# Samples' features finished block by block at the end of two SwiGLU down phases, and where their norms' products stand

## The chip, the cores and the metric

The kernel runs on one core of a Trainium2 chip. The core has TensorE (PE; PEld is its weight load), VectorE (DVE), ScalarE (ACT), GpSimd (POOL) and SyncE (SP, which only issues transfers), each with its own in-order instruction queue, and 16 DMA engines that all queues share. The metric is the device time of one execution in microseconds; the time before is the median of three runs.

## The reference

One decoder layer over 1024 prompt tokens and 8 samples of 4 tokens, in fp32. Three sublayers, each with a norm that is scaled and shifted per sequence, and a gated residual; then a final norm:

```python
h = _modulate(_rms(x, p["ffn1_norm"]), sh1, sc1)
x = x + 0.5 * g1[:, None, :] * _swiglu(h, p["ffn1_w_gate"], p["ffn1_w_up"], p["ffn1_w_down"])
h = _modulate(_rms(x, p["mix_norm"]), sh2, sc2)
m, new = _mixer(h, conv[l], hst[l], shift[l], wkv[l], p)
x = x + g2[:, None, :] * m
h = _modulate(_rms(x, p["ffn2_norm"]), sh3, sc3)
x = x + 0.5 * g3[:, None, :] * _swiglu(h, p["ffn2_w_gate"], p["ffn2_w_up"], p["ffn2_w_down"])
...
y = _rms(x, final_norm)
```

`_swiglu(h, wg, wu, wd)` is `(silu(h @ wg) * (h @ wu)) @ wd`; the model has 1024 features and 2816 hidden ones. `_rms` divides each token by the root of the mean of its squared features and multiplies by a vector. The gates g1, g2, g3 are one vector for the prompt and one for each of the eight samples. `_mixer` is a parallel pair of recurrences (RG-LRU and RWKV-7) between two projections, w_in and w_out.

## The kernel before

**Tiling.** x lies in the core's memory as features by tokens: 8 blocks of 128 features, and 1056 columns, of which the last 32 are the samples' tokens. In the phases spoken of here the columns are taken in three pieces, piece 0 and 1 of 384 columns and piece 2 of 288, that is 256 prompt columns and the 32 of the samples. Every product is fp32 made of three products of split operands (lines 61 to 63 in `mm3`): a value is split by ACT into a rounded high part (line 46) and by DVE into the rest (line 47).

**Order.** The program is written in Python and a planner puts each engine's instructions in order, by its own estimates of time and by priority, which is the written order unless a `high_priority` says otherwise. Inside `in_order(engine)` the engine keeps the written order. So PE's order in the last group of a down phase is as written, while DVE, ACT and POOL are planned. In most of the mixer PE is planned too.

**A down phase (`down`, line 475).** The hidden features come in groups of two or three blocks of 128 from DRAM. For each group, piece and block `ob` of output features, PE makes nine products (six in small groups) into one PSUM tile, `pd`. Then `acc_x` (lines 460 to 466) adds it to x on DVE: line 463 for the prompt columns, with the prompt's gate. The samples' 32 columns are only summed up in `sacc`, without a gate (line 466), since each sample has its own gate. In the last group the pieces go 0, 1, 2, and when all blocks of piece 2 are done, `add_samples` multiplies all of `sacc` (8 x 32 columns) by the gates (line 472) and adds it to x (line 473).

**The norm behind it (`rstd_steps`, line 166)** is a generator in three steps, so that its few products on PE can be put between those of the next piece. Step one: ACT squares each feature block (lines 173 and 176), and an adder engine (POOL in ffn1; in ffn2 POOL for pieces 0 and 1, DVE for piece 2) sums the blocks into `acc` (line 177; the profile names it nacc). For piece 2 this takes the 256 prompt columns, and the samples' columns come separately: one square over 8 x 32 columns (line 180) and one reduction on DVE (line 181). Step two: eight narrow products sum over features (line 185, `nps`), then a root on ACT (line 187) and a reciprocal on DVE (line 188). Step three: eight products spread the result over 128 rows (line 192, `npb`), copied to memory by ACT (line 194, `nrs`).

`done(ci)` runs step one as soon as a piece's blocks are written; the next two steps are taken while the next piece's blocks are written, behind the block numbers in `marks`. The line

```python
if pend and ob in marks[i - 1]:
    next(pend, None)
```

stands in the loop over blocks. The default `marks=((1, 3), (2, 4))` holds in ffn1's phase. The call of ffn2's phase gives its own, `((2, 4), (5, 7))`. Steps two and three for piece 2 of ffn1 are taken in the mixer's first projection, behind its second and third product group (`pj`).

**What follows.** In ffn1, step three is followed by the mixer's norm: DVE scales (line 436, `nt`), ACT adds the shift and rounds (line 443), DVE takes the rest (line 444); the samples' columns go through lines 455 to 457. Beside these, the projection's weights arrive by DMA through one buffer (`wr`) and are split. x is also stored to DRAM from POOL's queue (line 1316, `dx_move`). In ffn2 the final norm follows: `final` (line 1675) scales piece 0 on DVE (line 1694), piece 1 on POOL (ACT multiplies by the norm's vector, line 1685, and POOL by `nrs`, line 1692), and piece 2 on both, five blocks on DVE and three on POOL. After every second block an output DMA is issued, from SP and ACT in turn (line 1696). `add_samples` is also called at the end of the mixer's output projection (`w_out_end`).

Of the kernel before, what the change touches and what calls it, by code (L numbers as in the profile page):

```python
# [8 lines left out]
F32 = mybir.dt.float32  # L9
F32R = mybir.dt.float32r  # L10
AF = mybir.ActivationFunctionType
ALU = mybir.AluOpType
PSUM = bass.MemoryType.PSUM

D, NP, NB, TS = 1024, 1024, 8, 4
T = NP + NB * TS
KD = D // 128
# [4 lines left out]
PL = NP - 768  # L22
# [16 lines left out]
def trunk(tc, a):  # L39
    nc = tc.nc  # L40
# [93 lines left out]
    x = None  # L134
# [31 lines left out]
    def rstd_steps(ci, ps_, sp, adder=nc.vector):  # L166
        c, n = PIECES[ci]
        b = n // 4
        np_ = n if ci != 2 else PL
        acc = sp.tile([128, n], F32, tag="acc", name="nacc")  # L170
        for k in range(KD):
            if k == 0:
                nc.scalar.activation(acc[:, 0:np_], x[:, 0, c:c + np_], AF.Square)
            else:
                sq = sp.tile([128, n], F32, tag="sq", name="nsq")
                nc.scalar.activation(sq[:, 0:np_], x[:, k, c:c + np_], AF.Square)
                adder.tensor_tensor(acc[:, 0:np_], acc[:, 0:np_], sq[:, 0:np_], op=ALU.add)
        if ci == 2:
            sq = sp.tile([128, n], F32, tag="sq", name="nsqs")[:, 0:256].rearrange("p (k t) -> p k t", k=KD)
            nc.scalar.activation(sq, x[:, :, NP:T], AF.Square)  # L180
            nc.vector.tensor_reduce(acc[:, PL:n].unsqueeze(2), sq.rearrange("p k t -> p t k"), axis=mybir.AxisListType.X, op=ALU.add)
        yield
        ps = ps_([b, 4], "nps")
        for s in range(4):
            nc.tensor.matmul(ps[:, s:s + 1], acc[:, b * s:b * s + b], ones, start=(s == 0), stop=(s == 3))
        rn = sp.tile([128, 4], F32, tag="rn", name="rn")
        nc.scalar.activation(rn[0:b], ps, AF.Sqrt, bias=eps[0:b])
        nc.vector.reciprocal(rn[0:b], rn[0:b])
        yield
        pb = ps_([128, n], "npb")  # L190
        for s in range(4):
            nc.tensor.matmul(pb[:, b * s:b * s + b], rn[0:b, s:s + 1].to_broadcast([b, 128]), ident[0:b, 0:b], start=True, stop=True)
        rs = sp.tile([128, n], F32, tag="rs", name="nrs")
        nc.scalar.activation(rs, pb, AF.Copy)
        yield rs
# [264 lines left out]
    def acc_x(ps, ci, ob, g, gs):  # L460
        c, n = PIECES[ci]
        np_ = n if ci != 2 else PL
        nc.vector.scalar_tensor_tensor(x[:, ob, c:c + np_], ps[:, 0:np_], g[:, ob, 0:1], x[:, ob, c:c + np_],  # L463
                                       op0=ALU.mult, op1=ALU.add)
        if np_ < n:
            nc.vector.tensor_tensor(sacc[:, ob, :], ps[:, np_:n], sacc[:, ob, :], op=ALU.add)

    sacc = const.tile([128, KD, 32], F32, name="sacc")

    def add_samples(g):  # L470
        sv = sacc.rearrange("p k (b s) -> p k b s", b=NB)
        nc.vector.tensor_tensor(sv, sv, g[:, :, 1:9].unsqueeze(3).to_broadcast([128, KD, NB, TS]), op=ALU.mult)
        nc.vector.tensor_tensor(x[:, :, NP:T], x[:, :, NP:T], sacc, op=ALU.add)

    def down(pre, gc, dH, hid, more, done, hot=False, main_done=None, pieces=(0, 1, 2), marks=((1, 3), (2, 4))):
        nc.vector.memset(sacc, 0.0)
        started = ExitStack()
        started.enter_context(in_order(nc.sync))
        for gi, (g0, g1) in enumerate(GROUPS):
            if gi == 2:  # L480
                started.close()
            last = g1 == NH
            if last and main_done:
                main_done()
            from_ = (more, more) if gi % 2 == 0 else (hid, PL_["w"])
            hid_t, wd = [], []
            for m in range(g0, g1):
                r = PL_["wr"].tile([128, T], F32, "wr", "wr")
                nc.sync.dma_start(r, dH[m])
                hid_t.append([from_[0].tile([128, T], F32R, t, t) for t in ("fh", "fl")])  # L490
                split(r, *hid_t[-1])
                wd.append(weight(a[pre + "_w_down"][m], from_[1]))
            pend = None
            with in_order(nc.tensor) if last else ExitStack():
                for i, ci in enumerate(pieces if last else (2, 1, 0)):
                    c, n = PIECES[ci]
                    with tc.high_priority(3000) if last and hot and i > 0 else ExitStack():
                        for ob in range(KD):
                            ps = F([128, n], "pd")
                            mm3(ps, [(wd[j][0][:, 128 * ob:128 * ob + 128], wd[j][1][:, 128 * ob:128 * ob + 128],  # L500
                                      hid_t[j][0][:, c:c + n], hid_t[j][1][:, c:c + n]) for j in range(g1 - g0)])
                            acc_x(ps, ci, ob, gc, None)
                            if pend and ob in marks[i - 1]:
                                next(pend, None)
                    if last:
                        for _ in pend or ():
                            pass
                        with tc.high_priority(3000) if ci == 2 else ExitStack():
                            if ci == 2:
                                add_samples(gc)  # L510
                            pend = done(ci)
                            next(pend)
        return pend
# [1149 lines left out]
    with ExitStack() as ph:  # L1663
# [13 lines left out]
        def final(ci):  # L1677
            c, n = PIECES[ci]
            s_ = rstd_steps(ci, PY, sp, {"P": nc.gpsimd, "V": nc.vector}[{0: 'P', 1: 'P', 2: 'V'}[ci]])
            next(s_)  # L1680
            yo = hp.tile([128, KD, n], F32, f"yo{ci}", "yo")
            eng = {0: 'VVVVVVVV', 1: 'PPPPPPPP', 2: 'VPVVPVVP'}[ci]
            for k in range(KD):
                if eng[k] == "P":
                    nc.scalar.activation(yo[:, k], x[:, k, c:c + n], AF.Copy, scale=vec[:, V_NF + k:V_NF + k + 1])
            yield
            for r in s_:
                if r is None:
                    yield
            for k in range(KD):  # L1690
                if eng[k] == "P":
                    nc.gpsimd.tensor_tensor(yo[:, k], yo[:, k], r, op=ALU.mult)
                else:
                    nc.vector.scalar_tensor_tensor(yo[:, k], x[:, k, c:c + n], vec[:, V_NF + k:V_NF + k + 1], r, op0=ALU.mult, op1=ALU.mult)
                if k % 2 == 1:
                    (nc.sync, nc.scalar)[k // 2 % 2].dma_start(yT[:, k - 1:k + 1, c:c + n], yo[:, k - 1:k + 1])
# [68 lines left out]
```

## Time and profile before

| what | value |
|---|---|
| time, median of 3 runs | 2209.8 us (2209.15 to 2214.6) |
| profiled execution, its own time | 2204.8 us |
| its span from first to last instruction | 2203.0 us |
| PE busy | 2098.9 us, 95% |
| DVE busy | 1409.2 us, 64% |
| ACT busy | 743.2 us, 34% |
| POOL busy | 209.4 us, 10% |
| mean granted clock of PE | 0.977 |
| last product of ffn2's down phase | about 2185 us |

How to read the lines of the profile: a row of the timeline gives the start and the duration in microseconds, the engine, the line of the kernel, the operation, the tile written and those read, their shapes, how many such instructions stand in the row, and in square brackets the idle time of the engine before it with what ended it. Names are those of the program. Matmul durations overlap, since products are pipelined. A row of waits gives who waited for whom: microseconds in total, times, the longest. A row of busy time by stretches gives the stretch and its length, the busy time of PE, PEld, DVE, ACT and POOL with their instruction counts, the granted clock, the DMA engines' busy share and GB/s. A row of grouped instructions gives the count, the busy time, the mean of one in ns, and the idle time before them. The chain of waits is the work that ended last, followed back from the end.

### The profile page before, as it was taken

To read this page: it belongs to the slowest core of one execution; us is meant where nothing else is said; L and a number is where in the kernel's file an instruction comes from. 1 tells how busy PE (TensorE), PEld (TensorE's weight loads), DVE (VectorE), ACT (ScalarE), POOL (GpSimd) and SP (SyncE) were. 2 spreads that over 40 slices of the span, in tenths; PEclk is the share of its full clock that TensorE was granted. 3 is DMA by queue.
4 is the path that set the end of the run, shared out by engine and by line. 5 is a ranking of instruction groups with operands and counts; after the bars stand their busy time and mean duration, and the time that the engine had idled before them with its cause. 6 is when DMAs were issued, how large, how long until landed. Compare 5 with 4: busy or idle time off the path is not lost.

```text
span 2203.0 us, 41916 instructions
## 1 busy us (share of the span) xinstructions
PE 2098.9 (95%) x17209; PEld 1989.5 (90%) x17209; DVE 1409.2 (64%) x2954; ACT 743.2 (34%) x1289; POOL 209.4 (10%) x310
## 2 busy tenths in 40 slices
PE   6899999999999999999998899879999999999997
PEld 4899999999999998898886689879999999999997
DVE  5855555565865565775855775687666666585655
ACT  5633232333311135443342441264333333331213
POOL 0000000000000041214230000100000000100004
PEclk8999999999999999999998999889999999999998
DMA  7244444442732212347576765431222222362312
GB/s 253 88 152 144 140 148 140 136 148 90 251 107 73 84 67 65 87 117 163 122 177 157 190 173 143 140 125 69 83 75 77 83 79 73 123 205 74 109 37 79
DMA packets 148414, 266.80 MB, mean 121 GB/s; under 512 B 76272, under 2 KB 92800, under 8 KB 146176
## 3 DMA queue, kind: packets, MB, share of 16 engines
q1 hardware_dynamic: 102656, 172.03, 25.1%
q0 software_dynamic: 19184, 63.14, 9.1%
q10 hardware_dynamic: 26384, 28.96, 5.6%
q8 instruction: 135, 2.21, 0.4%
q14 instruction: 55, 0.45, 0.1%
HBM read 200.20 MB, written 63.82 MB: 120 GB/s over the span
## 4 chain that ended last, share of the span: by engine, by line
PE 76%; DVE 10%; DMA 3%; issue 3%; ACT 3%; POOL 1%; SPq 1%; ACTq 0%; DVEq 0%; POOLq 0%
PE pd L61 7%; PE pd L62 7%; PE pd L63 7%; PE pX L61 4%; PE pZ L61 4%; PE pX L62 4%; PE pZ L63 4%; PE pX L63 4%; PE pW L61 4%; PE pW L63 4%; PE pW L62 4%; PE pZ L62 4%; PE pY L63 2%; PE pY L61 2%; PE pY L62 2%
## 5 line engine op out<-in xcount | busy, mean ns | idle before, releaser
L61 PE MATMUL pd<-fl,wh 128*128 128x384 f32 (+1 forms) x1056 | 340.9, 326 | 3.5 <-DVE fl L47 2.6
L63 PE MATMUL pd<-fh,wh 128*128 128x384 f32 (+1 forms) x1056 | 341.4, 324 | 0.0
L62 PE MATMUL pd<-fh,wl 128*128 128x384 f32 (+1 forms) x1056 | 341.4, 324 | 0.0
L46 ACT ACTIVATE wh<-wr 128x512 fp32r<-128x512 f32 (+1 forms) x254 | 192.1, 761 | 254.5 <-PE pZ L63 71.7
L47 DVE TENSOR_TENSOR wl<-wr,wh 128x512 fp32r<-128x512 f32 (+1 forms) x254 | 215.0, 851 | 89.8 <-ACT wh L46 84.3
L61 PEld LDWEIGHTS pd<-fl,wh 128*128 128x128 f32 x1056 | 198.9, 189 | 5.2 <-ACT wh L46 2.7
L62 PEld LDWEIGHTS pd<-fh,wl 128*128 128x128 f32 x1056 | 199.7, 189 | 0.0
L63 PEld LDWEIGHTS pd<-fh,wh 128*128 128x128 f32 x1056 | 199.4, 189 | 0.0
L61 PE MATMUL pW<-t,wh 128*128 128x266 f32 (+1 forms) x640 | 182.6, 285 | 0.0
L63 PE MATMUL pW<-t,wh 128*128 128x266 f32 (+1 forms) x640 | 182.3, 285 | 0.0
L62 PE MATMUL pW<-t,wl 128*128 128x266 f32 (+1 forms) x640 | 182.2, 285 | 0.0
L463 DVE SCALAR_TENSOR_TENSOR x<-pd,g3c,x 128x384 f32<-128x384 f32 (+1 forms) x192 | 107.0, 568 | 83.1 <-PE pd L63 83.1
L463 DVE SCALAR_TENSOR_TENSOR x<-pd,g1c,x 128x384 f32<-128x384 f32 (+1 forms) x192 | 107.4, 567 | 76.7 <-PE pd L63 76.6
L419 ACT ACTIVATE e<-e,bt 128x262 f32<-128x262 f32 x80 | 41.3, 516 | 293.8 <-DVE bt L418 274.2
L344 POOL DMA_DIRECT2D dh<-hf x88 | 48.0, 545 | 972.4 <-DVE hf L425 793.9
L46 ACT ACTIVATE fh<-wr 128x1056 fp32r<-128x1056 f32 x44 | 47.5, 1082 | 243.2 <-PE pd L63 193.7
L62 PEld LDWEIGHTS pW<-t,wl 128*128 128x128 f32 x640 | 120.8, 189 | 0.0
L61 PEld LDWEIGHTS pW<-t,wh 128*128 128x128 f32 x640 | 120.5, 188 | 0.0
L63 PEld LDWEIGHTS pW<-t,wh 128*128 128x128 f32 x640 | 120.5, 188 | 0.0
L47 DVE TENSOR_TENSOR wl<-s,wh 128x512 fp32r<-128x512 f32 x120 | 82.6, 689 | 55.3 <-ACT wh L46 55.2
L416 DVE TENSOR_TENSOR e<-pZ,e 128x266 f32<-128x266 f32 x80 | 34.4, 430 | 104.3 <-PE pZ L63 104.1
L46 ACT ACTIVATE wh<-s 128x512 fp32r<-128x512 f32 x120 | 75.4, 629 | 65.9 <-PE pW L63 31.4
(495 smaller groups left out, 5888.8 us busy)
## 6 DMA issues: line engine op xcount, KB each, us to landing
wa<-in_w_ada SPq DMA_DIRECT2D x72, 512.0 KB, 3.9
dh<-hf POOLq DMA_DIRECT2D x88, 264.0 KB, 2.3
wr<-dh SPq DMA_DIRECT2D x44, 528.0 KB, 4.3
wr<-in_ffn_w_gate SPq DMA_DIRECT2D x44, 512.0 KB, 3.5
wr<-in_ffn_w_up SPq DMA_DIRECT2D x44, 512.0 KB, 3.5
wr<-in_ffn_w_down SPq DMA_DIRECT2D x44, 512.0 KB, 4.2
ch<-dc ACTq DMA_DIRECT2D x32, 512.0 KB, 6.5
wr<-in_w_in SPq DMA_DIRECT2D x22, 512.0 KB, 3.9
```

Source lines behind the costliest of these rows:

```text
L46: nc.scalar.activation(hi, raw, AF.Copy)
L47: nc.vector.tensor_tensor(lo, raw, hi.bitcast(F32), op=ALU.subtract)
L61: nc.tensor.matmul(ps, wh, xl, start=(first and i == 0), stop=False, **kw)
L62: nc.tensor.matmul(ps, wl, xh, start=False, stop=False, **kw)
L63: nc.tensor.matmul(ps, wh, xh, start=False, stop=(last and i == n - 1), **kw)
L344: nc.gpsimd.dma_start(self.dH[m][:, 528 * p:528 * p + 528], hf)
L416: tt(g2, pz, u, op=ALU.add)
L419: nc.scalar.activation(g2[:, 0:n], g2[:, 0:n], AF.Silu, bias=bt[:, 0:1])
L463: nc.vector.scalar_tensor_tensor(x[:, ob, c:c + np_], ps[:, 0:np_], g[:, ob, 0:1], x[:, ob, c:c + np_], op0=ALU.mult, op1=ALU.add)
```

## The change

Four edits, in lines 166 to 190, 470 to 512 and 1680.

1. Samples' features are finished block by block: `add_samples` takes a range of blocks, and in the last group it is called behind each block of piece 2 (128 x 32 columns) instead of once behind all of them. Called for all blocks, as at the end of w_out, it works in two halves of four blocks.
2. The sums of squares of piece 2 run over all 288 columns, like those of the other pieces; the separate square and reduction of the samples' columns (lines 179 to 181) are gone.
3. The default marks become `((3, 5), (3, 5))`: behind which blocks of the next piece a norm's two product groups stand. ffn2's call keeps `((2, 4), (5, 7))`.
4. In the final norm all eight blocks of piece 2 are scaled on DVE; POOL and ACT's scalings for it are gone. Pieces 0 and 1 stay as they are.

```diff
     def rstd_steps(ci, ps_, sp, adder=nc.vector):
         c, n = PIECES[ci]
         b = n // 4
-        np_ = n if ci != 2 else PL
         acc = sp.tile([128, n], F32, tag="acc", name="nacc")
         for k in range(KD):
             if k == 0:
-                nc.scalar.activation(acc[:, 0:np_], x[:, 0, c:c + np_], AF.Square)
+                nc.scalar.activation(acc, x[:, 0, c:c + n], AF.Square)
             else:
                 sq = sp.tile([128, n], F32, tag="sq", name="nsq")
-                nc.scalar.activation(sq[:, 0:np_], x[:, k, c:c + np_], AF.Square)
-                adder.tensor_tensor(acc[:, 0:np_], acc[:, 0:np_], sq[:, 0:np_], op=ALU.add)
-        if ci == 2:
-            sq = sp.tile([128, n], F32, tag="sq", name="nsqs")[:, 0:256].rearrange("p (k t) -> p k t", k=KD)
-            nc.scalar.activation(sq, x[:, :, NP:T], AF.Square)
-            nc.vector.tensor_reduce(acc[:, PL:n].unsqueeze(2), sq.rearrange("p k t -> p t k"), axis=mybir.AxisListType.X, op=ALU.add)
+                nc.scalar.activation(sq, x[:, k, c:c + n], AF.Square)
+                adder.tensor_tensor(acc, acc, sq, op=ALU.add)
         yield
...
-    def add_samples(g):
-        sv = sacc.rearrange("p k (b s) -> p k b s", b=NB)
-        nc.vector.tensor_tensor(sv, sv, g[:, :, 1:9].unsqueeze(3).to_broadcast([128, KD, NB, TS]), op=ALU.mult)
-        nc.vector.tensor_tensor(x[:, :, NP:T], x[:, :, NP:T], sacc, op=ALU.add)
-
-    def down(pre, gc, dH, hid, more, done, hot=False, main_done=None, pieces=(0, 1, 2), marks=((1, 3), (2, 4))):
+    def add_samples(g, k0=0, k1=KD):
+        for a_, b_ in ((k0, min(k1, 4)), (max(k0, 4), k1)):
+            if a_ < b_:
+                h = slice(a_, b_)
+                sv = sacc[:, h].rearrange("p k (b s) -> p k b s", b=NB)
+                nc.vector.tensor_tensor(sv, sv, g[:, h, 1:9].unsqueeze(3).to_broadcast([128, b_ - a_, NB, TS]), op=ALU.mult)
+                nc.vector.tensor_tensor(x[:, h, NP:T], x[:, h, NP:T], sacc[:, h], op=ALU.add)
+
+    def down(pre, gc, dH, hid, more, done, hot=False, main_done=None, pieces=(0, 1, 2), marks=((3, 5), (3, 5))):
...
                             acc_x(ps, ci, ob, gc, None)
+                            if last and ci == 2:
+                                add_samples(gc, ob, ob + 1)
                             if pend and ob in marks[i - 1]:
                                 next(pend, None)
...
                         with tc.high_priority(3000) if ci == 2 else ExitStack():
-                            if ci == 2:
-                                add_samples(gc)
                             pend = done(ci)
                             next(pend)
...
-            eng = {0: 'VVVVVVVV', 1: 'PPPPPPPP', 2: 'VPVVPVVP'}[ci]
+            eng = {0: 'VVVVVVVV', 1: 'PPPPPPPP', 2: 'VVVVVVVV'}[ci]
```

## The prediction

> **What bounds the kernel now.** I read the page first, then PE's waits around the end of the first down phase, then that stage's busy times and timeline, then the last 20 us. Of the page:
>
> ```profile
> span 2203.0 us, 41916 instructions
> PE 2098.9 (95%) x17209; PEld 1989.5 (90%) x17209; DVE 1409.2 (64%) x2954; ACT 743.2 (34%) x1289; POOL 209.4 (10%) x310
> PE 76%; DVE 10%; DMA 3%; issue 3%; ACT 3%; POOL 1%; SPq 1%; ACTq 0%; DVEq 0%; POOLq 0%
> ```
>
> TensorE sets the time; the change removes no product, so it can win only where PE waits beside the edited lines. There are two such places: the end of ffn1's down phase and the tail behind ffn2's. PE's waits from 780 to 850 us, then the busy time of every engine (PE, PEld, DVE, ACT, POOL) by stretches of that stage:
>
> ```profile
> PE nps L185 <- POOL nacc L177: 3.1, 1, 3.1
> PE nps L185 <- DVE nacc L181: 2.1, 1, 2.1
> ...
> 799.07:816.00 16.93, 13.85 (x86) 13.62 (x85) 16.17 (x31) 8.23 (x17) 8.59 (x9) 0.90 0.29 94
> 816.00:833.10 17.10, 14.44 (x94) 14.01 (x93) 15.96 (x34) 8.99 (x17) 6.66 (x7) 0.97 0.27 87
> ```
>
> PE stands still twice, both times ahead of the product that sums the squares (nps, L185). But DVE is busy for 16.17 + 15.96 = 32.13 of the 34.03 us, idle 1.9: whatever PE saves here, DVE must be able to follow. The instructions that matter, from the timeline:
>
> ```profile
> 793.30 0.80 PE L185 MATMUL nps<-ones,nacc 128*96 128x1 f32 x8
> 797.22 1.03 PE L192 MATMUL npb<-ident,rn 96*128 96x96 f32 x8
> 799.07 2.39 DVE L436 SCALAR_TENSOR_TENSOR nt<-x,sc,nrs 128x384 f32<-128x384 f32 x3 [1.03 <-ACT nrs L194]
> 811.20 1.02 PE L185 MATMUL nps<-ones,nacc 128*96 128x1 f32 x8 [3.08 <-POOL nacc L177]
> 812.95 0.44 PE L61 MATMUL pd<-fl,wh 128*128 128x288 f32 x1
> 813.19 0.44 PE L62 MATMUL pd<-fh,wl 128*128 128x288 f32 x1
> 815.11 0.30 PE L61 MATMUL pd<-fl,wh 128*128 128x288 f32 x1
> 826.81 0.41 DVE L472 TENSOR_TENSOR sacc<-sacc,g1c 128x256 f32<-128x256 f32 x1
> 828.24 0.41 DVE L473 TENSOR_TENSOR x<-x,sacc 128x256 f32<-128x256 f32 x1
> 830.44 1.15 DVE L47 TENSOR_TENSOR wl<-wr,wh 128x1024 fp32r<-128x1024 f32 x1
> 831.52 0.56 DVE L181 TENSOR_REDUCE nacc<-nsqs 128x32 f32<-128x256 f32 x1
> 832.13 0.38 PE L185 MATMUL nps<-ones,nacc 128*72 128x1 f32 x2 [2.13 <-DVE nacc L181]
> 834.11 0.52 PE L63 MATMUL pj<-h1h,wh 128*128 128x384 f32 x1
> 835.84 0.34 PE L63 MATMUL pj<-h1h,wh 128*128 128x384 f32 x1
> 831.62 5.62 DMA wr<-in_w_in
> 837.26 1.06 ACT L46 ACTIVATE wh<-wr 128x1024 fp32r<-128x1024 f32 x1 [4.46 <-DMA wr<-in_w_in]
> 838.35 1.23 DVE L47 TENSOR_TENSOR wl<-wr,wh 128x1024 fp32r<-128x1024 f32 x1 [5.13 <-ACT wh L46]
> 839.15 0.41 ACT L194 ACTIVATE nrs<-npb 128x288 f32<-128x288 f32 x1 [0.84 <-PE npb L192]
> 839.60 0.43 DVE L455 TENSOR_TENSOR nts<-x,nrs 128x256 f32<-128x256 f32 x1
> ```
>
> Between the first nps and npb of piece 0 lie two blocks of nine products: (797.22 - 793.30 - 0.80)/18 = 0.173 us each at 384 columns, so 0.13 at 288. After the long wait they come 0.24 apart (812.95, 813.19), and last 0.44 instead of 0.30; after the second wait 0.52 instead of 0.34. This holds for 2.9 us (811.20 + 1.02 to 815.11) and for up to 3.3 (832.13 + 0.38 to 835.84). At about half pace that loses 1.5 and 1.6 us on top of the 3.08 and 2.13. The last norm's work on DVE (L455, 839.60) starts on two paths that end together: nrs on ACT (839.15 + 0.41 = 839.56), which hangs on PE, and the fourth weight's split that stands ahead of it on DVE (838.35 + 1.23 = 839.58), which hangs on the third split (830.44) through one buffer and a DMA of 5.62.
>
> **The change, part by part.** Four rows of DVE for the prices:
>
> ```profile
> 2178.36 0.17 DVE L466 TENSOR_TENSOR sacc<-pd,sacc 128x32 f32<-128x32 f32 x1
> 2178.46 0.47 DVE L463 SCALAR_TENSOR_TENSOR x<-pd,g3c,x 128x256 f32<-128x256 f32 x1
> 2171.32 4.66 DVE L1694 SCALAR_TENSOR_TENSOR yo<-x,vec,nrs 128x384 f32<-128x384 f32 x8 [1.54 <-ACT nrs L194]
> 1438.34 0.41 DVE L472 TENSOR_TENSOR sacc<-sacc,mod 128x256 f32<-128x256 f32 x1
> ```
>
> *Later products (ffn1 only; ffn2's call hands over marks of its own).* nps and npb of piece 0 move from behind blocks 1 and 3 of piece 1 to behind 3 and 5. Between nps and npb (793.30, 797.22) lie two blocks and the nps itself, 3.92 - 0.8 = 3.1 us: so the norm's scaling starts on DVE at 802.2 instead of 799.07. In that time DVE does two accumulations that it would otherwise do later, 0.55 each (between L463's 0.47 at 256 columns and L1694's 4.66/8 = 0.58 at 384): 3.1 - 1.1 = +2.0 us for a queue that is full until 833.1. For piece 1 the nps goes one block later (block 2 to 3): PE's 3.08 shrinks by one block, 9 x 0.13 = 1.2 us. If the wait vanishes, 3.08 + 1.5 go; if POOL's sum moves with DVE's 2.0, nothing goes. DVE's 1.9 idle is hidden behind these waits and is what it can win back: net +0.1 on DVE, bounds -1.9 and +2.0.
>
> *Samples' features block by block.* Away: L472, L473 and L181. New: 16 operations of 128 x 32 in place of two of 128 x 256. Their nearest row is L466, and what it costs the queue is the distance to the next start (2178.36, 2178.46): 0.10 each, 1.6 in all, less 0.41 + 0.41 + 0.56: +0.2 us of DVE per down phase (16 x 0.17 would make it +1.3). VectorE: DVE Perf Modes in the Trainium skill, section "Rules for kernel authors", speaks against this part: it says to keep the number of operations small, since each one is followed by a drain. The trace agrees that the count matters: 0.10 for an eighth of the width that takes 0.41, sixteen times. The 16 stand behind the accumulation that waits for the same block, so they add no wait of their own; behind them queue only the norm's scalings, and POOL's store of x, which waited for L473, is issued sooner. What is won is order: the last sample column is ready with block 7, so the 2.13 wait for L181 goes, and with it 1.6 of slow products: -3.7 for PE. Next late would be the last h1 (its split is in the DVE queue to 833.1), which PE needs some 4 us after nps: covered.
>
> What comes through: if the fourth weight stays ahead of L455 on DVE, the start at 839.6 moves with the third split alone, by DVE's +0.1 + 0.2 = +0.3, and PE's gain is hidden; if the planner puts it behind, nrs rules and -3.7 comes through. Nothing in the trace says which; I take the middle, -1.7. In w_out's end the two sample operations become four (the 1438.34 row): between 4 x 0.10 and 4 x 0.41 against 0.82: -0.4 to +0.8, taken +0.2. The squares over 288 columns instead of 256 cost ACT and the adder under 0.05 each.
>
> *The tail.* Last operations, with the shapes' group of POOL and the DMA rate in 0.5 us slices from 2184:
>
> ```profile
> 2186.23 0.41 ACT L176 ACTIVATE nsq<-x 128x256 f32<-128x256 f32 x1
> 2186.33 0.42 DVE L177 TENSOR_TENSOR nacc<-nacc,nsq 128x256 f32<-128x256 f32 x1
> 2186.41 11.34 POOL L1692 TENSOR_TENSOR yo<-yo,nrs 128x384 f32<-128x384 f32 x11 [5.76 <-DVE sacc L472]
> 2186.66 1.21 DVE L473 TENSOR_TENSOR x<-x,sacc 128x256 f32<-128x256 f32 x1
> 2187.80 1.22 DVE L177 TENSOR_TENSOR nacc<-nacc,nsq 128x256 f32<-128x256 f32 x1
> 2192.70 5.36 DVE L1694 SCALAR_TENSOR_TENSOR yo<-x,vec,nrs 128x288 f32<-128x288 f32 x5 [2.31 <-ACT nrs L194]
> ...
> L1692 POOL TENSOR_TENSOR yo<-yo,nrs 128x384 f32<-128x384 f32 x8 | 8.4, 1094 | 5.8 <-DVE sacc L472 5.8
> ...
> GB/s 0 0 0 0 0 0 0 0 0 0 0 252 362 172 0 160 378 249 0 243 366 178 0 0 0 154 364 313 364 370 362 346 346 362 164 0 0 0 0 0
> ```
>
> Once POOL works (2186.41), DVE's two-input operations take 1.21 and 1.22 where the same took 0.41. L473 stands between the sixth and the last sum of squares: without it the last one starts at 2186.7 and ends, still at POOL's pace, at 2187.9 instead of 2189.0: -1.1 (-1.9 if it ran at 0.42; -0.3 if the sum before it is caught too). All behind it moves along, so the scaling starts at 2191.6. POOL now has piece 1 alone: 2186.41 + 8.4 = 2194.8. Until then DVE does three at 5.36/5 = 1.07; the other five I price by L1694's 0.58 at 384 columns with POOL quiet, times 288/384 = 0.44: end at 2197.0 against 2192.70 + 5.36 = 2198.06, -1.1. ACT's three scalings for POOL fall away; the four output DMAs stay, behind DVE instead of POOL. At 0.58 each it is -0.4, with a start at -1.9 it is -1.4; if DVE stays at 1.07 for all eight, 2200.2, +2.1. GPSIMD Engine Reference in the Trainium skill, "8. Key points", says that GpSimd shares SBUF interfaces with VectorE and contends with its instructions of two SBUF inputs; the trace agrees (1.21 against 0.41), and by it the 1.07 ends with POOL. The output then follows: the DMA runs full (about 360 GB/s) from 2196.5 to 2201.5, and piece 2's first pairs come 1 to 2 us sooner, so the end moves with the last scaling.
>
> Sum: -1.7 + 0.2 - 1.1 = -2.6 us; span 2200.4. The profiled execution took 2204.8 with 1.8 us around its span, so it would be 2202.2; it stood 5.0 under the median of 2209.8, whose runs go from 2209.15 to 2214.6, so on the median I forecast **2207.2**. About 0.3%, 6.6 us, is what a measurement can tell here.
>
> **Rivals.** *Both waits really end* (chance 0.22). DVE follows, the fourth weight moves behind: both waits with their slow products are worth 3.08 + 1.5 + 3.7 = 8.3, but L455 can't start before the DVE queue ends, 833.1 - 1.9 + 0.2 = 831.4, and npb and nrs (1.03 + 0.41) have run: 832.8 instead of 839.6, -6.8; with +0.2 and -1.1 it is -7.7, so 2202.1. For: both waits have work to fill them. Against: DVE is 94% busy.
>
> *Later marks starve DVE* (0.17). DVE idles 2.0 longer ahead of a full queue, POOL's sum comes as much later, the third split and its DMA too: +2.0 + 0.2 in ffn1, +0.8 in w_out, and the tail's -1.1: +1.9, so 2211.7, slower than before. It decides as soon as the 1.9 idle isn't won back.
>
> *The planner reorders the mixer* (0.13). PE's order there isn't written out; PE's longest waits between 850 and 1440 us are these, and one more or one fewer of this kind is 4.7 either way, two in a row 9:
>
> ```profile
> PE pd L957 <- ACT X L947: 4.8, 4, 3.5
> PE ptY L1028 <- DVE yc L995: 4.6, 1, 4.6
> ```
>
> So 2202 to 2216; nothing in the profile favours a sign.
>
> *DVE is slow in the tail for another reason than POOL* (0.06): +2.1 in place of -1.1, total +0.6: 2210.4. Against it: L1694 ran at 0.58 with POOL quiet.
>
> **How the numbers follow.** My forecast has 0.42, its own range 2204 to 2210.5 (ffn1 -3.7 to +0.3, w_out -0.4 to +0.8, tail -1.4 to -0.4). Faster by over 0.3%: most of the first rival, a third of the planner's, little of the forecast's: 0.24. Slower by over 0.3%: two fifths of the planner's and a rest of the second rival: 0.09. Else 0.67. Range 2200 to 2214: the first rival's 2202 and the second's 2211.7 lie inside, with 2 us beyond for the planner.
>
> **What will show it.** Right: no L181, the nps of piece 2 in ffn1 without idle time and full-pace products behind it; L455's start between 836 and 840; the tail's last sum of squares without an operation of L473 ahead of it and 1.1 sooner behind PE's last block; first three scalings near 1.07, the last five near 0.44. Wrong: a longer wait at the second nps of ffn1, a DVE queue that ends after 834, all eight scalings near 1.07, or a mixer whose length changes by more than 5 us.

## The result, and the profile after

| what | before | after |
|---|---|---|
| time, median | 2210.8 us of 4 runs (2209.15 to 2214.6) | 2232.9 us of 4 runs (2226.8 to 2233.4) |
| ratio of the times, 95% interval | | 1.009 (1.007 to 1.011) |
| span of the profiled execution | 2203.0 us | 2231.4 us |
| PE busy | 2098.9 us | 2111.0 us |

The changed kernel is slower by some 22 us. The prediction said 2207.2, between 2200 and 2214, and was wrong. The page of the changed kernel, the lines that answer to those shown of before:

```profile
span 2231.4 us, 41933 instructions
...
PE 2111.0 (95%) x17209; PEld 2000.2 (90%) x17209; DVE 1414.5 (63%) x2985; ACT 741.1 (33%) x1284; POOL 205.8 (9%) x307
...
PE 76%; DVE 8%; DMA 5%; issue 4%; ACT 3%; SPq 1%; POOL 0%; ACTq 0%; DVEq 0%; POOLq 0%
```

PE runs the same 17209 matmuls and still ends 28 us later in its profiled execution (before's, 2204.8 us, lies 6 under its median; after's, 2233.4, at its median); in the chain of waits DMA and "issue" have risen by two and one hundredths. No share says where. So I cut the span at four instructions that both kernels have: the first square of piece 0 in ffn1's norm, the samples' scaling (`nts`, L455 of before, L450 of after), the first product of the last norm group ahead of ffn2 (`nps` x12), and the last product of ffn2's down phase. The times of the cuts are starts of rows of the timeline.

| stage (us) | before | after | difference |
|---|---|---|---|
| start to the first square (no edit yet) | 780.1 | 782.3 | +2.2 |
| ffn1's norm: first square to `nts` | 59.6 | 61.0 | +1.5 |
| mixer and ffn2's norm: `nts` to `nps` x12 | 626.2 | 649.1 | +23.0 |
| ffn2: `nps` x12 to its last product | 718.9 | 721.6 | +2.7 |
| tail: last product to the end | 18.4 | 17.4 | -0.9 |

The first row holds no edit. The fourth holds only the samples' small operations on DVE beside ffn2's last blocks, and the kernels below that leave ffn2 as it was show 718.7 to 721.6 there too. The 23 us lie in the mixer, whose only edited operations are the two for the samples at its end, which became four. Busy time by stretches for the mixer (columns: stretch and length, busy time of PE, PEld, DVE, ACT, POOL with counts, granted clock, DMA share, GB/s), before:

```profile
839.60:1465.75 626.15, 579.05 (x5819) 515.34 (x5818) 422.30 (x961) 242.33 (x406) 103.43 (x157) 0.95 0.56 143
```

and after:

```profile
843.29:1492.40 649.11, 586.28 (x5812) 521.45 (x5811) 422.74 (x964) 242.00 (x406) 103.54 (x157) 0.94 0.55 138
```

DVE, ACT and POOL work as long as before. PE is idle 649.1 - 586.3 = 62.8 us instead of 47.1, and its products take 7.2 us longer at a slightly lower granted clock. PE's waits of after in the mixer (total, times, longest):

```profile
PE po L61 <- DVE h0ly L47: 6.6, 1, 6.6
...
PE pw L938 <- DMA ch<-dc: 5.9, 1, 5.9
PE ptY L1026 <- DVE yc L993: 5.8, 2, 4.6
PE pw L938 <- issue: 5.3, 2, 4.0
```

Of these before has only that for `yc`. Apart from those two operations the mixer has the same instructions in both kernels. Yet the planner put 2261 of PE's 4039, 513 of DVE's 922, 194 of ACT's 456, 28 of POOL's 146 and 47 of SP's 129 in other places, up to 85 places away on PE. (Counted in the two programs, instruction by instruction.)

At the end of ffn1, PE's waits from 780 to 850 us:

```profile
PE pj L62 <- DVE wl L47: 3.4, 1, 3.4
PE pj L61 <- ACT wh L46: 2.8, 1, 2.8
...
PE nps L180 <- POOL nacc L176: 0.9, 1, 0.9
```

The two waits for the norm's sums, 3.1 and 2.1 us, have shrunk to one of 0.9. In their place PE waits 6.2 us for the projection's split weights. From the timeline there, with the first square:

```profile
782.26 0.53 ACT L172 ACTIVATE nacc<-x 128x384 f32<-128x384 f32 x1 [26.22 <-DVE x L458]
...
835.76 0.62 PE L180 MATMUL nps<-ones,nacc 128*72 128x1 f32 x8
835.83 1.21 DVE L47 TENSOR_TENSOR wl<-wr,wh 128x1024 fp32r<-128x1024 f32 x1
842.02 0.39 ACT L189 ACTIVATE nrs<-npb 128x288 f32<-128x288 f32 x1
842.14 1.23 DVE L47 TENSOR_TENSOR wl<-wr,wh 128x1024 fp32r<-128x1024 f32 x1 [2.74 <-ACT wh L46]
843.29 0.42 DVE L450 TENSOR_TENSOR nts<-x,nrs 128x256 f32<-128x256 f32 x1
```

The small operations of after from 800 to 845 us, in the view of groups (count, busy time, mean of one in ns, idle time before them):

```profile
L471 DVE TENSOR_TENSOR x<-x,sacc 128x32 f32<-128x32 f32 x8 | 2.6, 333 | 0.0
...
L470 DVE TENSOR_TENSOR sacc<-sacc,g1c 128x32 f32<-128x32 f32 x8 | 1.3, 167 | 0.0
```

The tail: in before, the first square of ffn1's norm and the last product of ffn2's down phase,

```profile
780.05 0.52 ACT L173 ACTIVATE nacc<-x 128x384 f32<-128x384 f32 x1 [26.61 <-DVE x L463]
...
2184.65 0.29 PE L63 MATMUL pd<-fh,wh 128*128 128x288 f32 x1
```

and that product with what follows it in after:

```profile
2213.96 0.29 PE L63 MATMUL pd<-fh,wh 128*128 128x288 f32 x1
2215.72 8.62 POOL L1690 TENSOR_TENSOR yo<-yo,nrs 128x384 f32<-128x384 f32 x8 [5.77 <-ACT nrs L189]
2216.01 2.24 DVE L176 TENSOR_TENSOR nacc<-nacc,nsq 128x288 f32<-128x288 f32 x2
2221.80 4.99 DVE L1692 SCALAR_TENSOR_TENSOR yo<-x,vec,nrs 128x288 f32<-128x288 f32 x8 [2.31 <-ACT nrs L189]
```

Two theories, A and B, stood at the start of the experiments, and a third, C, came with `e8`. A: the planner's other order of the mixer costs the time, and the edits themselves are worth +1.5 us in ffn1 and -0.9 in the tail. B: the edits cost it, because the mixer starts later against its transfers and against POOL, whatever the order. C: the marks are what makes it slow.

### The profile page after: what moved, and what is told of

Same layout as the page of the kernel before. It is cut to its first block, busy times and chain, and to the rows that moved or that the text cites. A ratio compares the mean times of both kernels' runs of the same rounds, so it can differ in the third digit from the quotient of the medians.

```text
span 2231.4 us, 41933 instructions
## 1 busy us (share of the span) xinstructions
PE 2111.0 (95%) x17209; PEld 2000.2 (90%) x17209; DVE 1414.5 (63%) x2985; ACT 741.1 (33%) x1284; POOL 205.8 (9%) x307
## 4 chain that ended last, share of the span: by engine, by line
PE 76%; DVE 8%; DMA 5%; issue 4%; ACT 3%; SPq 1%; POOL 0%; ACTq 0%; DVEq 0%; POOLq 0%
PE pd L61 7%; PE pd L62 7%; PE pd L63 7%; PE pX L61 4%; PE pZ L61 4%; PE pX L62 3%; PE pZ L63 3%; PE pX L63 3%; PE pW L61 3%; PE pW L63 3%; PE pW L62 3%; PE pZ L62 3%; PE pY L63 2%; PE pY L61 2%; PE pY L62 2%
```

## Experiments

### The order alone, in both directions

A list of each engine's mixer instructions is added, and behind every one a dependency that only fixes the order:

```diff
+    traced = {i.name: i for i in nc.cur_bb.bb.instructions}
+    for seq in ORDER:                      # PE, DVE, ACT, POOL, SP
+        for p_, q_ in zip(seq, seq[1:]):
+            tc.add_manual_dep(traced[f"I-{q_}"], f"I-{p_}", mybir.DependencyInfo(mybir.DependencyClass.NoSync, mybir.DependencyReason.DATA), reason="order")
     es.close()
```

`e1` is the whole change with the mixer in before's order:

> The whole change, but the mixer's instructions are held, on all five engines, in the order among themselves that the kernel before has (4039 on PE, 922 on DVE, 456 on ACT, 146 on POOL, 129 on SP; the same work). Theory A (the planner's other order of the mixer costs the time, and the edits themselves are worth +1.5 us at the first down phase and -0.9 us in the tail): the mixer, from the start of its norm's scalings to ffn2's first norm product, is back at 627 us, not 650, and the time is about 2211 us, 2208 to 2214. Theory B (the edits themselves cost it: the norm that ends later, or the marks, shift the mixer against its transfers and against POOL, whatever the order): mixer 645 us or more and the time 2225 to 2233.

`e2` is the kernel before with the mixer in the changed kernel's order:

> The kernel before, with none of the change's edits, but its mixer is held in the order that the changed kernel has. Theory A (order): the mixer takes about 650 us and the time is 2229 to 2233 us, with the tail as before (18.6 us from the last down product to the end). Theory B (edits): mixer 627 us and 2208 to 2213 us, as before.

Measured: `e1` 2212.2 us, ratio to before 1.0005 (0.9992 to 1.0019); `e2` 2231.7 us, 1.0099 (1.0074 to 1.0124). The mixer in `e1`:

```profile
844.40:1470.09 625.69, 577.57 (x5806) 514.36 (x5804) 422.50 (x964) 242.29 (x406) 103.58 (x157) 0.95 0.57 143
```

and in `e2`:

```profile
841.40:1487.72 646.32, 591.77 (x5816) 525.95 (x5814) 422.90 (x962) 242.01 (x406) 103.19 (x157) 0.93 0.55 138
```

With every edit in place and the old order, nothing is lost, so the added dependencies cost nothing that shows either; with no edit and the new order, all of it is lost. Theory A holds on both sides, and B falls: in `e1` the mixer starts at 844.4, later than in the changed kernel, and still takes 625.7. Of the new waits, PE's in `e2` from 1260 to 1345 us:

```profile
PE po L68 <- DVE h0ly L54: 4.2, 1, 4.2
PE pw L947 <- issue: 4.0, 1, 4.0
```

They belong to the order, then. (Line numbers of a kernel with such a list are 7 higher.)

### The parts of the change

`e3` is the tail's part alone. In ffn2's down phase the samples come block by block, the sums run over 288 columns, and all scalings of piece 2 are on DVE:

```diff
+                            if last and hot and ci == 2:
+                                add_block(gc, ob)
...
-            eng = {0: 'VVVVVVVV', 1: 'PPPPPPPP', 2: 'VPVVPVVP'}[ci]
+            eng = {0: 'VVVVVVVV', 1: 'PPPPPPPP', 2: 'VVVVVVVV'}[ci]
```

> The change's edits in ffn2's down phase and the last norm alone: samples' features finished block by block, sums of squares over all 288 columns, all eight scalings on VectorE. ffn1 and the mixer are as before, and the mixer's order is that of before. Theory A: mixer 627 us, last down product to the end 18.6 to 17.7 us (17.3 to 18.2), time 2209.5 us, 2207.5 to 2211, that is 0.9 us or 0.04% under before. Theory B says the same of this kernel, as ffn1 is untouched. If POOL's writes of the results or two-input additions that run at the slow price of 1.07 us eat the gain, the stretch is 18.5 us or more and the time is that of before or over it.

Measured: 2210.8 us, ratio 0.9991 (0.9974 to 1.0007); tail 17.3 us against 18.4. Its profiled execution was the longest of its ten (2216.6 us), and its mixer took 634.5 us in the same order as before's 626.2: one profile of the mixer is uncertain by some 9 us, and only medians of several runs decide there.

`e4` is the marks alone:

```diff
-    def down(pre, gc, dH, hid, more, done, hot=False, main_done=None, pieces=(0, 1, 2), marks=((1, 3), (2, 4))):
+    def down(pre, gc, dH, hid, more, done, hot=False, main_done=None, pieces=(0, 1, 2), marks=((3, 5), (3, 5))):
```

> The marks alone, (3, 5) and (3, 5) for (1, 3) and (2, 4): the products of a piece's norm placed behind later blocks; all else is as before. The planner's own order is left free here and places 1083 of PE's 4039 mixer instructions otherwise than before. Theory A (order): the time follows the mixer's length and nothing else, of either sign; the norm's own end before the mixer moves by under 3 us. From the one changed order that was seen (+23 us with 2261 displaced) an estimate by share is +11 us, with -10 to +25 as bounds. Theory B (the marks shift or starve DVE): +2 to +23 us, with the loss already there at the start of the mixer's scalings or growing evenly through the mixer.

Measured: 2224.0 us, ratio 1.0054 (1.0032 to 1.0075), mixer 640.4 us, ffn1's norm 59.6 us as before. In ffn1 itself no cost of the marks is seen.

`e8` is the change without the marks:

```diff
-    def down(pre, gc, dH, hid, more, done, hot=False, main_done=None, pieces=(0, 1, 2), marks=((3, 5), (3, 5))):
+    def down(pre, gc, dH, hid, more, done, hot=False, main_done=None, pieces=(0, 1, 2), marks=((1, 3), (2, 4))):
```

> The whole change but its marks, which stay at (1, 3) and (2, 4); the planner's own order of the mixer is left free and differs from before's in 2018 of PE's 4039 places. Theory A (order): slower by an amount of its own, by share of displaced products +18 us (the whole change has 2261 and +20, the marks alone 1083 and +12), bounds 0 and +25; the ffn1 stretch, from the first square of piece 0 to the samples' scaling nts, 59 to 61 us as before's 59.6. Theory C (the marks are what makes the planner's order worse): 2208 to 2214 us, as before.

Measured: 2227.7 us, ratio 1.0061 (1.0046 to 1.0077), mixer 643.0 us, ffn1's norm 61.0 us. Theory C falls: with or without the marks the planner finds a slower order. The +1.5 in ffn1 is there without them, so it belongs to the other edits.

### Where in the mixer

I compared the time of each product in `e2` with that of the same product in before. This lag is 3.4 us at 900 us (medians over the 20 us that follow), 4.7 at 1000, 9.8 at 1060, 13.7 at 1180, 14.8 at 1240, 27.0 at 1300 and 22.3 at 1420: between 1240 and 1300 it grows most, and a part of that is made up behind. (The 13.8 and 21.8 that the expectation of `e7` names for this stretch do not come out of the traces so.) `e5`, `e6` and `e7` are the kernel before with the new order in one part only: up to 1180 us in before's trace, behind it, and from 1265 to 1340.

```diff
+ORDER = (    # before's own order; in the part named, the changed kernel's
...
+)
```

The dependencies are those shown above.

> The kernel before, with the mixer's instructions held in the changed kernel's order where they start before 1180 us in the trace of before, and in their own order behind that (1157 of PE's 4039 stand otherwise). Theory A1 (the loss is the sum of separate places, each its own displaced work): the lag that the products of the run with the whole new order show against before at 1180 us, 13.7 us less the 3.4 that it starts with, comes through: mixer 637 us (627 + 10), time about 2222 us. Theory A2 (the loss comes from one place in the second half, the wait of w_out's first products for h0ly and of the chunk's product pw, and the rest is recovered): mixer 627 to 629, time 2211 to 2214.

> The mirror image: before's order up to 1180 us, the changed kernel's order behind it (1104 of PE's 4039). Theory A1 (separate places, losses add): the rest of the lag, 22.3 - 13.7 = 8.6 us, comes through: mixer 635.5 us, time about 2220.5, and the two halves together make the 20 us of the whole. Theory A2: 640 us or more here alone. A third way, a shift in the first half that sets off all that follows: mixer 627 to 629.

> The kernel before, with the changed kernel's order only among the instructions that start between 1265 and 1340 us in the trace of before (451 of PE's 4039, 110 of DVE's 922, 59 of ACT's 456): there PE's wait for the chunk's product pw (4.0 us) and for the split h0ly (4.2 and 6.6 us) appear with the new order, and the lag grows from 13.8 to 21.8 us. Theory A1: this stretch alone costs 7 to 8 us, mixer 634.5 us, time about 2219.5, and both waits are there. If the waits come from something ahead of the stretch, they are absent and the mixer takes 627 to 630 us.

Measured: 2222.0, 2224.1 and 2220.2 us, that is 1.0041 (1.0026 to 1.0057), 1.0052 (1.0034 to 1.0069) and 1.0030 (1.0018 to 1.0042). The halves together make 0.93%, the whole 0.99%. So the loss is a sum of separate places (A1), and one stretch, 75 us long, holds a third of it. There before has these rows (PE's `pd`, `py` and `pw` are steps of a recurrence by chunks; `St` and `ch` on DVE lie between them):

```profile
1277.21 0.68 PE L957 MATMUL pd<-X,ch 128*64 128x64 f32 x14
...
1279.62 0.42 DVE L959 TENSOR_TENSOR St<-pd,pc 128x256 f32<-128x256 f32 x1
1283.54 0.86 DVE L963 TENSOR_TENSOR ch<-St,Sd 64x256 f32<-64x256 f32 x2
1285.61 0.69 PE L940 MATMUL pw<-ch 128*64 128x64 f32 x16
...
1290.89 0.32 ACTq L1604 DMA_DIRECT2D yr<-dy  x1
```

and `e7` these:

```profile
1289.77 0.68 PE L964 MATMUL pd<-X,ch 128*64 128x64 f32 x14
1293.80 0.42 DVE L966 TENSOR_TENSOR St<-pd,pc 128x256 f32<-128x256 f32 x1
1295.06 0.54 ACTq L1611 DMA_DIRECT2D yr<-dy  x1
1296.81 0.86 DVE L970 TENSOR_TENSOR ch<-St,Sd 64x256 f32<-64x256 f32 x2
1297.32 1.30 PE L947 MATMUL pw<-ch 128*64 128x64 f32 x16 [3.99 <-issue]
1304.51 0.52 ACT L53 ACTIVATE h0hy<-yr 128x384 fp32r<-128x384 f32 x1 [4.12 <-DMA yr<-dy]
1305.67 0.69 PE L68 MATMUL po<-h0ly,wh 128*128 128x384 f32 x1 [4.41 <-DVE h0ly L54]
```

The load of `yr`, a source of w_out's products, from its issue to its landing in before and in `e7` (shortest, median and longest of one):

```profile
DMA to landing us min/median/max: 4.2/4.2/4.2
...
DMA to landing us min/median/max: 9.4/9.4/9.4
```

From `pd` to `pw` it is about as long in both: 8.4 and 7.6 us. In before PE fills it with products of a projection and waits for nothing. In `e7` those products come ahead of `pd`, which starts 9.1 us later when each is counted from its mixer's start (839.60 and 843.10), and only 12 of w_out's (`po`) are left to fill the time; the wait of 3.99 at `pw` is the rest, although it is labelled "issue". The next `po` then needs `h0ly`, whose source `yr` is loaded by a DMA: 4.41 more. ACT's queue issues that load as far behind the mixer's start as in before (452.0 and 451.3 us), but it lands 9.4 us later instead of 4.2. In `e7` four loads of the next step (`ch` and `X`, 1292.56 to 1294.36) stand ahead of it in ACT's queue, which before issues behind it, from 1297.36 on; that they are what makes it slow was not tested. Neither wait has an added instruction behind it.

`e9` tests this by the least move. Fourteen instructions (28 in the trace), `pd` and `py` of one step, go behind the projection's products:

```diff
 order on PE (times of before)
-1277.21 pd x14, py x14
 1278.4  pj ... (46 products)
+        pd x14, py x14
 1285.61 pw x16
```

> The kernel before, its mixer held in its own order but for 14 of PE's 4039 instructions (28 in the trace): one chunk step's state products (pd x14 and py x14, at 1277.21 us in the trace of before) move behind the projection's products that follow them, to just ahead of the chunk's next product pw at 1285.61. No work is added. Theory A: the recurrence's chain from pd over DVE (St, then ch) to pw is fixed, 1277.89 to 1284.40 in before, of which St to the end of ch is 4.8 us; with no products left to fill it PE waits 4.3 us ahead of pw, and DVE's queue behind St comes 5 us later: the time rises by 4 to 8 us, to 2217 to 2221. If a shift of so few products is absorbed by the queues, 2210 to 2214.

Measured: 2220.0 us, ratio 1.0041 (1.0027 to 1.0055), mixer 634.9 us. The rows of `e9`:

```profile
1291.50 0.68 PE L964 MATMUL pd<-X,ch 128*64 128x64 f32 x14
...
1296.65 1.52 PE L947 MATMUL pw<-ch 128*64 128x64 f32 x16 [3.87 <-issue]
```

Moving 14 of 4039 products costs 8.7 us by the medians (0.41%; the interval is 6 to 12 us). The mixer's length of one profile can't bear that out: 634.9 is hardly above the 634.5 that `e3` showed in before's order. The wait itself is 3.9, near the 4.3 expected. The products behind that wait run slow as well: `pw` x16 takes 1.52 us against 0.69, and the 17 of `po` behind it 5.0 (1298.10 to 1303.08) against 3.3 in before (1286.23 to 1289.55). With these it is some 6 us; where the rest comes from isn't shown.

### How sensitive the planner's order is

`e11` and `e12` shift marks by one block in the kernel before: `((1, 3), (2, 5))`, and `((2, 4), (2, 4))`.

```diff
-    def down(pre, gc, dH, hid, more, done, hot=False, main_done=None, pieces=(0, 1, 2), marks=((1, 3), (2, 4))):
+    def down(pre, gc, dH, hid, more, done, hot=False, main_done=None, pieces=(0, 1, 2), marks=((1, 3), (2, 5))):     # e12: ((2, 4), (2, 4))
```

> The kernel before with the smallest change of its marks: the second norm's second product group behind block 5 instead of 4, that is eight narrow products 1.2 us later. The planner, left free, then places 2345 of PE's 4039 mixer products otherwise. Theory A: again 8 to 25 us slower, since the order of before is an unusually good one and three other orders of the planner cost 12 to 20; the ffn1 stretch within 1 us of 59.6. If orders are good or bad with equal chance, -10 to +10. Without the order nothing in this edit is worth over 1 us.

> The kernel before with marks (2, 4) and (2, 4): the first norm's first product group one block later. The planner places 1357 of PE's 4039 mixer products otherwise. Theory A: 5 to 20 us slower for the order alone, ffn1 stretch within 1 us of 59.6. If orders are good or bad with equal chance, -10 to +10.

Measured: `e11` 2237.1 us, ratio 1.0125 (1.0107 to 1.0142), mixer 657.8, ffn1's norm 59.6; `e12` 2222.8 us, 1.0063 (1.0046 to 1.0079), ffn1's norm 59.9. Eight narrow products placed one block later cost 26 us. The mixer is where the profile shows it, and the planner's order there is the one thing known to differ; but before's order was not held in this kernel, so that it is the order is argued from `e1` and `e2`. `e12`'s profiled execution was its fastest (2216.7 us, mixer 634.1), so its place of loss isn't shown, only its ratio.

### The tail, and ffn1's +1.5

In the tail DVE's two last sums took 2.24 us together while POOL worked. `e10` is `e3` with piece 1's scalings on DVE too, so that POOL is quiet:

```diff
-            eng = {0: 'VVVVVVVV', 1: 'PPPPPPPP', 2: 'VVVVVVVV'}[ci]
+            eng = {0: 'VVVVVVVV', 1: 'VVVVVVVV', 2: 'VVVVVVVV'}[ci]
```

> The tail part alone, as in the run with the tail's edits only, and piece 1's eight scalings on DVE too instead of ACT and POOL, so that POOL does nothing in the last 17 us. The mixer's order is that of before. Theory P (POOL's work is what makes DVE's two-input operations slow): the last two sums of squares take 0.45 us each, not 1.1, and all of piece 2's scalings 0.44; DVE has 8 x 0.58 = 4.7 us more to do, of which about 4 fit into its waits for the norm: last down product to the end 15.8 us (15.3 to 17.3) against 17.3, time about 2209. If DVE takes piece 1's scalings ahead of the sums, 19 us or more; if the sums stay at 1.1 with POOL quiet, theory P is wrong.

Measured: 2210.7 us, ratio 0.9998 (0.9986 to 1.0011), tail 18.3 us. Its last rows on DVE:

```profile
2198.19 2.73 DVE L1702 SCALAR_TENSOR_TENSOR yo<-x,vec,nrs 128x384 f32<-128x384 f32 x5
2200.84 0.45 DVE L177 TENSOR_TENSOR nacc<-nacc,nsq 128x288 f32<-128x288 f32 x1
2201.20 1.67 DVE L1702 SCALAR_TENSOR_TENSOR yo<-x,vec,nrs 128x384 f32<-128x384 f32 x3
2202.79 0.46 DVE L177 TENSOR_TENSOR nacc<-nacc,nsq 128x288 f32<-128x288 f32 x1
...
2207.44 3.52 DVE L1702 SCALAR_TENSOR_TENSOR yo<-x,vec,nrs 128x288 f32<-128x288 f32 x8 [2.52 <-ACT nrs L194]
```

With POOL quiet the sums take 0.45 and the eight scalings 3.52, that is 0.44 each: POOL's work is what makes them slow. The Trainium skill, GPSIMD Engine Reference, "8. Key points", names such contention for DVE's instructions with two SBUF inputs; the rows agree and give it a price, 2.24 / 2 against 0.45. The gain was lost to the order of DVE's queue: the planner put all of piece 1's scalings ahead of the last sums, the case that the expectation named as a possibility but with too high a price.

`e14` fixes that order, three of piece 1's scalings behind the last sum and five behind the reciprocal:

```diff
+    for j, i in enumerate(fin["p1"]):      # piece 1's eight scalings
+        tc.add_manual_dep(i, fin["sum" if j < 3 else "rn"].name, mybir.DependencyInfo(mybir.DependencyClass.NoSync, mybir.DependencyReason.DATA), reason="order")
```

> The tail's edits, piece 1's eight scalings on DVE as in the run with POOL quiet, but in a fixed place: three behind the last sum of squares, five behind the reciprocal of piece 2's norm. The mixer's order is that of before. If DVE's order is what ate that run's gain: sums at 0.45 us, the last one ended 3.5 us behind the start of PE's last down product (7.4 in that run), all sixteen scalings at 0.58 and 0.44, last down product to the end 15.0 us (14.5 to 16) against 18.3 in before, time 2208 us, ratio 0.9985 (0.997 to 1.000). If the output transfers are the bound instead (3.1 MB at 360 GB/s are 7.7 us from the first pair), 17 us or more.

Measured: 2209.7 us (12 runs, before 2211.3), ratio 0.9990 (0.9978 to 1.0002); the tail is 2212.6 - 2197.92 = 14.7 us, as expected. (The 7.7 us of the expectation's other branch are 8.6 by its own figures, 3.1 MB at 360 GB/s.) Its rows, from PE's last down product on:

```profile
2197.92 0.29 PE L63 MATMUL pd<-fh,wh 128*128 128x288 f32 x1
...
2200.31 1.03 DVE L179 TENSOR_TENSOR nacc<-nacc,nsq 128x288 f32<-128x288 f32 x2
2201.25 1.67 DVE L1706 SCALAR_TENSOR_TENSOR yo<-x,vec,nrs 128x384 f32<-128x384 f32 x3
...
2202.93 6.13 DVE L1706 SCALAR_TENSOR_TENSOR yo<-x,vec,nrs 128x384 f32<-128x384 f32 x13
```

Its median is 1.6 us under that of before on the same chip, and the trace shows 3.7 us less tail, the shortest of the kernels tried. The interval of the times still touches 1, so a gain in time isn't shown; the mixer's spread from run to run is larger than 3.7.

`e13` asks whether ffn1's +1.5 comes from the sixteen small operations. The samples are finished in two halves, without the marks' change:

```diff
-                            if last and ci == 2:
-                                add_samples(gc, ob, ob + 1)
+                            if last and ci == 2 and (hot or ob % 4 == 3):
+                                add_samples(gc, ob if hot else ob - 3, ob + 1)
```

> The whole change but for its marks, and in ffn1 the samples' features are finished in two halves of four blocks (behind blocks 3 and 7, four operations of 128 x 128) instead of block by block (sixteen of 128 x 32). The sums over 288 columns stay. The mixer's order is the planner's own (2372 of PE's 4039 stand otherwise than in before), so the time, by the other such orders 2220 to 2240 us, tells nothing; what is asked is the ffn1 stretch from the first square of piece 0 to the samples' scaling nts, 59.2 to 60.8 us in kernels without the edit (mean 59.7) and 61.0 with sixteen operations. If the sixteen are the cause: 59.7 to 60.3. If it is the wide sums on POOL or the work's place: 60.8 to 61.3.

Measured: 2234.8 us (two runs; yet another order), ffn1's norm 62.4 us, above both expectations. The rows of `e13`:

```profile
779.82 0.53 ACT L172 ACTIVATE nacc<-x 128x384 f32<-128x384 f32 x1 [26.53 <-DVE x L458]
...
831.06 1.53 DVE L47 TENSOR_TENSOR wl<-wr,wh 128x1024 fp32r<-128x1024 f32 x1
834.36 0.68 PE L180 MATMUL nps<-ones,nacc 128*72 128x1 f32 x8 [4.13 <-POOL nacc L176]
...
842.20 0.42 DVE L450 TENSOR_TENSOR nts<-x,nrs 128x256 f32<-128x256 f32 x1 [3.21 <-ACT nrs L189]
```

Counted from the first square, the third weight's split comes at 50.4 us in before, at 53.1 in `e8` with sixteen operations and at 51.2 here with four (831.06 - 779.82). Kernels without edits 1 and 2 in ffn1 show 50.1 to 51.7, so that delay goes with the sixteen operations. But now four blocks' samples arrive at once, POOL's sums over 288 columns stand behind them, and PE waits 4.1 us for the last; `nts` waits for `nrs`. So both of the things asked about can hold the end of this stage. That the sixteen operations alone make the 1.5 isn't shown.

## Why the prediction was wrong

**The frame.** "It can win only where PE waits beside the edited lines" was taken for the whole effect, and the sum, -1.7 + 0.2 - 1.1, has no term for the mixer's order; the runs put that term at +20 us (`e2`) and everything else at about 0 (`e1`, 1.0005). The sentence is no bound on what the change can lose: the planner orders the mixer by its own estimates, and every edit of ffn1 that was tried gave it another plan. The prediction's own sign for that, "a mixer whose length changes by more than 5 us", is what showed it.

**The rival that came true was mis-sized, and its chance too low.** "The planner reorders the mixer" stood with 0.13 and a price of "4.7 either way, two in a row 9", 2202 to 2216 (9 either way would be 2198 to 2216; the range of the forecast stops at 2214). The mechanism was right. The size was off, 20 us by `e2`, because I took one wait of the mixer as the unit and at most two of them; the halves show a sum of separate places, and one move of 14 products is already worth 6 to 12 (`e9`). "Nothing in the profile favours a sign" stood as well; six other orders (the change, `e4`, `e8`, `e11`, `e12`, `e13`) were all slower, by 11 to 26 us, though only the first was tried apart from its edits. Why before's order is better than all six stays open; the trace of before alone could not have told it.

**ffn1, predicted -1.7, measured +1.5 (61.0 - 59.6; +2.7 in `e1`).** The size is rough: kernels without edits 1 and 2 in ffn1 took 59.1 to 60.8 us there (`e14` and `e10`), the three with both, block by block, 61.0 to 62.2. A loss of 1 to 2 us is likely, a gain of 1.7 excluded. The fork was right: the fourth weight stayed ahead of L450 on DVE, its split ended at 842.14 + 1.23 = 843.37 and `nts` began at 843.29. In that branch the prediction had +0.3. What failed is the size of DVE's extra work: "0.10 each, 1.6 in all" for the sixteen operations; they were busy 2.6 + 1.3 = 3.9 us, single ones up to 0.8 where a sum of POOL's ran beside them. The third split began 835.83 - 782.26 = 53.6 us behind the first square instead of 50.4, and 1.5 of these 3.2 us came through. That the operations alone do it isn't shown, as `e13` says. The warning of the Trainium skill, VectorE: DVE Perf Modes, "Rules for kernel authors", against a high count of operations was named and then priced by the quiet row alone; the trace agrees with it, 3.9 us busy for the sixteen against 0.41 + 0.41 + 0.56 for the three that went.

**The waits.** The wait for L181 went, as predicted, and the one for POOL shrank from 3.1 to 0.9, by the 2.1 that lie between the two cases given. "1.6 of slow products" were to go with it; PE waited 2.8 and 3.4 us for weights instead. The scaling of piece 0 started 21.8 us behind the first square instead of 19.0, 2.8 later (3.1 predicted). That the marks cost DVE next to nothing agrees with `e4`, 59.6.

**The tail, predicted -1.1, measured -0.9, and 1.0 in `e3` and 1.3 in `e1`: right in sum, not in its parts.** The start of the scaling moved by (2221.80 - 2213.96) - (2192.70 - 2184.65) = -0.2 instead of -1.1, since POOL caught both last sums, the case that stood at -0.3. The eight scalings took 4.99 where before's five took 5.36 (5.4 predicted): two at 1.2 and six at 0.43 for three at 1.07 and five at 0.44. The rest, 0.3, is a shorter way from the last scaling to the end, which I had set to nothing. w_out's four operations lie 0.33 apart, before's two 0.45: 4 x 0.33 - 2 x 0.45 = +0.4 against +0.2, inside the bounds.

**Starved DVE** as a rival has no support: the marks alone leave ffn1's norm as it was, and the change in before's order is at 1.0005.

## What to carry to other kernels

Where a planner orders part of a program, an edit ahead of that part is two changes: price the edit by its own rows, and price the new order apart from it, by holding the old one and timing both. A recurrence with a fixed length is hidden only by what stands behind its first step in the queue; so ask of each long chain which independent work its engine still has at that moment, and write that order out once it is good. A rival of small places that add up must be sized by their number, not by the longest wait.

## What the runs showed that I had not expected

Fourteen instructions moved behind 46 others cost 8.7 us by the medians (6 to 12) without any work added, more than the wait that they make (3.9 us). The same order of the mixer took 625.7 to 634.5 us in five profiled executions (before, `e1`, `e3`, `e10`, `e14`), and the new one 646.3 and 649.1, so a single profile could not have told an effect of 5 us there. And a wait that the table of waits puts down to "issue" was, by the rows beside it, a wait for DVE's `ch`, which was still being written (1296.81, 0.86 us for two) as `pw` began at 1297.32.
